# A mixture-of-experts kernel: two loads of x with their rows interleaved, and ScalarE's copy of h in two instructions for two experts

## The chip, the cores and the metric

The kernel runs on one core of one Trainium2 chip. A core has TensorE (PE) for matrix products, whose results lie in PSUM; ScalarE (ACT) and VectorE (DVE), which read PSUM and SBUF; GpSimd (POOL) and SyncE (SP), which here only issue transfers and pass on semaphores; and 16 DMA engines, which move data between HBM and SBUF. SBUF and PSUM have 128 partitions. The metric is the device time of one execution in microseconds: the median of the runs shown, before the change 180.69 us.

## The reference

Eight experts, each with 256 rows of x, 512 hidden columns and 2048 columns in between; everything is float32:

```python
n_experts, capacity, hidden, expert_hidden = 8, 256, 512, 2048
h = np.matmul(x, w1) + b1[:, np.newaxis, :]
h = np.maximum(h, 0)
out = np.matmul(h, w2) + b2[:, np.newaxis, :]
```

The weights w1 and w2 are 4 MB each for an expert, 64 MB in all, and the kernel reads each once.

## The kernel before

**Stages.** The kernel is written out by hand inside one critical section; each engine has its own list of instructions and they meet at semaphores. There are 11 stages, s = 0 to 10 (E + LAG, with LAG = 3). In stage s TensorE computes the first layer of expert s (for s below 8), and after it the second layer of expert s - 3 (from s = 3 on). The first layer is 16 rows of h (the loop over j; a row is here a block of 128 of the 2048 columns of h, transposed, for all 256 rows of x), each of four matmuls into one of four PSUM banks `ph`; the second layer is 32 matmuls into two banks `po`.

**Loads.** All weights are loaded by GpSimd, which converts them to fp16 on the way (`load_w1`, `load_w2`, lines 147 to 163), three buffers for w1 and three for w2 (NW). The order is fixed at lines 165 to 176: w1 of expert 0, b2, w1 of 1, x of 2 and 3, w1 of 2, w1 of 3, w2 of 0, x of 4 to 7, w1 of 4, w2 of 1, and so on. From expert 3 on, a load of w1 waits until TensorE has done the first layer that read the buffer (`s_ph`), and a load of w2 until the second layer is done (`s_po`). x of experts 0 and 1 alone comes as float32, in two transfers that SP issues before the critical section (line 131), ahead of the first weights: GpSimd's first load waits for a semaphore that ScalarE gives after its first small activation (line 127). SP then passes on, stage by stage, that x has been transposed and that weights have landed (`go`, lines 235 to 237 and 249 to 276), and TensorE takes that at line 282. Two stores of several experts' results and two of one expert's are issued by SP near the end (`flush`, `store`).

**x of experts 0 and 1.** 256 rows of 512 numbers lie one behind the other in HBM. Before the change partition p gets the two rows 2p and 2p + 1, which is 4 KB. (The change's short description counts such pairs of rows as one row.) VectorE casts expert 0 to fp16 and transposes it, ScalarE casts expert 1 (lines 133 to 135). `transposes` brings x to `xT` with 32 x 32 blocks; the columns of `xT` come in the order (row within the partition r, partition i).

**ScalarE's copy of h.** Line 224 adds the bias, takes the maximum with 0 and writes a row of h as fp16 into `hT`, and counts up `s_credit`; TensorE starts a row only with a credit, so it can be four rows ahead. The columns of `ph` are in the order of `xT`, and those of `hT` have to be in an order in which the results of a group of experts can be stored in long pieces (`GROUPS`: four experts together, then two). `h_columns` (line 206) gives the two access patterns, source and destination, for that. For experts 0 to 3 a partition of the group's result holds 8 rows (S), while a partition of x holds two rows (R) for experts 0 and 1, four for 2 and 3.

Of the kernel before, what the change touches and what calls it, by code (L numbers as in the profile page):

```python
# [10 lines left out]
def kernel(  # L11
# [12 lines left out]
    nc = tc.nc  # L24
    fp32 = mybir.dt.float32
    fp16 = mybir.dt.float16
    relu = mybir.ActivationFunctionType.Relu
    PE = mybir.EngineType.PE
    E, T, H = x.shape
    M = w1.shape[2]  # L30
    P = 128
    nTB = T // P
# [4 lines left out]
    B = 32  # L37
    nB = P // B
    LAG = 3
    NW = 3  # L40
    NPH = 4
    GROUPS = {0: 4, 4: 2}
# [6 lines left out]
    def sbuf(name, shape, dtype):  # L49
        return ctx.enter_context(nc.sbuf_tensor(name, shape, dtype))  # L50

    def sem(name):
        return ctx.enter_context(nc.semaphore(name=name))
# [3 lines left out]
    warm = sbuf("warm", [1, P], fp16)  # L57
    b2_sb = sbuf("b2_sb", [1, (LAG + E) * H], fp16)
    b1_rows = sbuf("b1_rows", [E * nB, M // nB], fp32)
    b1T = sbuf("b1T", [P, nJ * B + nB - 1], fp32)  # L60
    w1_sb = sbuf("w1_sb", [P, NW * nKC * M], fp16)
    w2_sb = sbuf("w2_sb", [P, NW * nJ * H], fp16)
    xT = sbuf("xT", [P, 2 * nKC * T], fp16)
    hT = sbuf("hT", [P, (LAG + 1) * nJ * T], fp16)
    x32 = [sbuf(f"x32_{e}", [P, nTB, H], fp32) for e in range(2)]
# [4 lines left out]
    for first, n in X_LOADS.items():  # L70
        R = n * T // P
# [9 lines left out]
    ph = ctx.enter_context(nc.psum_tensor("ph", [P, NPH, H], fp32))  # L81
# [5 lines left out]
    def load(engine, key, **kw):  # L87
        landed[key] = sem(f"d_{key}")
        engine.dma_start(**kw).then_inc(landed[key], 16)  # L89
# [4 lines left out]
    s_credit = sem("ph_free")  # L94
# [14 lines left out]
    def transposes(e):  # L109
# [19 lines left out]
        out=b1_rows[:], in_=b1.rearrange("e (b i) -> (e b) i", b=nB)))  # L129
    for e in range(2):  # L130
        tc.keep_in_program_order(nc.sync.dma_start(
            out=x32[e][:], in_=x[e].rearrange("(p tb) h -> p tb h", tb=nTB)))
    nc.vector.tensor_copy(out=x16[0][0][:], in_=x32[0][:])  # L133
    transposes(0)
    tc.keep_in_program_order(nc.scalar.copy(out=x16[1][0][:], in_=x32[1][:]))  # L135
# [12 lines left out]
    def load_w1(e):  # L148
        if e >= NW:
            nc.gpsimd.wait_ge(s_ph, nJ * (e - NW + 1))  # L150
        at = e % NW * nKC * M
        load(nc.gpsimd, f"w1_{e}",
             out=w1_sb[:, at : at + nKC * M].rearrange("p (kc m) -> p kc m", kc=nKC),
             in_=w1[e].rearrange("(p kc) m -> p kc m", kc=nKC))

    def load_w2(e):
        if e >= NW:
            nc.gpsimd.wait_ge(s_po, nTB * (e - NW + 1))
        dst = w2_sb[:, e % NW * nJ * H : (e % NW + 1) * nJ * H].rearrange("p (j h) -> p j h", j=nJ)
        src = w2[e].rearrange("(p j) h -> p j h", j=nJ)  # L160
        cuts = CUTS.get(e, (0, nJ))
        for lo, hi in zip(cuts, cuts[1:]):
            load(nc.gpsimd, f"w2_{e}_{lo}", out=dst[:, lo:hi], in_=src[:, lo:hi])

    nc.gpsimd.wait_ge(s_first, 1)
    load_w1(0)
    load(nc.gpsimd, "b2", out=b2_sb[:, LAG * H :],
         in_=b2.rearrange("e h -> (e h)").rearrange("(o f) -> o f", o=1))
    for s in range(1, E + LAG - 1):
        if s < E:  # L170
            if s in X_LOADS:
                load_x(s)
            load_w1(s)
        if s >= LAG:
            load_w2(s - LAG)
    load_w2(E - 1)
# [3 lines left out]
    for b in range(nB):  # L180
        turned = nc.vector.transpose(  # L181
            out=b1T[b * B : (b + 1) * B, nB - 1 - b : nB - 1 - b + nJ * B],
            in_=b1_rows[:].rearrange("r (i j) -> r j i", j=nJ),
# [3 lines left out]
    def evict(e, tb):  # L187
        engine = nc.vector if tb else nc.scalar
        copy = nc.vector.tensor_copy if tb else nc.scalar.copy
        first, n = group_of.get(e, (e, 1))  # L190
        rows = P // n
        at = (e - first) * rows
        engine.wait_ge(s_po, nTB * e + tb + 1)
        for k in range(n):
            bank = (e % 2 * nTB + tb) * H
            last = copy(out=results[e][at : at + rows, tb * n + k, :],  # L196
                        in_=po[k * rows : (k + 1) * rows, bank : bank + H])
        last.then_inc(s_out[tb], 1)
# [6 lines left out]

    def h_columns(e, dst, src):
        R, S = x16[e][2], group_of.get(e, (e, 1))[1] * nTB
        if R >= S:
            return (dst.rearrange("p (k i v) -> p k i v", k=S, v=R // S),
                    src.rearrange("p (v k i) -> p k i v", k=S, v=R // S))  # L210
        return (dst.rearrange("p (u r i) -> p u r i", r=R, u=S // R),
                src.rearrange("p (r i u) -> p u r i", r=R, u=S // R))

    nc.scalar.wait_ge(s_b1, 1)
    for s in range(E + LAG):
        if s < E:
            if s > LAG:
                nc.scalar.wait_ge(s_po, nTB * (s - LAG))
            for j in range(nJ):
                h_at = (s % (LAG + 1) * nJ + j) * T  # L220
                dst, src = h_columns(s, hT[:, h_at : h_at + T], ph[:, j % NPH, 0:T])
                bias_at = j * B + s * nB + nB - 1
                nc.scalar.wait_ge(s_ph, nJ * s + j + 1)
                nc.scalar.activation(  # L224
                    out=dst,
                    in_=src,
                    func=relu,
                    bias=b1T[:, bias_at : bias_at + 1],
                    scale=1.0,
                ).then_inc(s_credit, 1)  # L230
        if s >= LAG:
            evict(s - LAG, 0)

# [15 lines left out]
    for s in range(E + LAG):  # L249
# [5 lines left out]
        e = s - LAG  # L255
# [28 lines left out]
    def at(value, most):  # L284
        return nc.tensor.snap(value.with_bounds(min_val=0, max_val=most))

    with nc.Fori(0, E + LAG, 1, engines=[PE]) as s:
        nc.tensor.wait_ge(s_credit, NPH)
        w_at = at(s % NW * (nKC * M), (NW - 1) * nKC * M)
        with nc.tensor.If(s < E):  # L290
            x_at = at(s % 2 * (nKC * T), nKC * T)
            take(s_go)
            with nc.Fori(w_at, w_at + nJ, half, engines=[PE]) as w_from:
                w_from = w_from.with_bounds(min_val=0, max_val=(NW - 1) * nKC * M + half)
                for j in range(half):
                    for kc in range(nKC):
                        last = nc.tensor.matmul(  # L297
                            ph[:, j % NPH, 0:T],
                            w1_sb[:, bass.ds(w_from + (kc * M + j), P, nJ)],
                            xT[:, bass.ds(x_at + kc * T, T)],  # L300
                            start=(kc == 0),
                            stop=(kc == nKC - 1),
                        )
# [4 lines left out]
        with nc.tensor.If(s >= LAG):  # L308
            h_at = at((s + 1) % (LAG + 1) * (nJ * T), LAG * nJ * T)
# [3 lines left out]
            def second(tb, h_from, w2_from, j, stop=False):  # L313
                return nc.tensor.matmul(  # L314
                    banks[tb],
                    hT[:, bass.ds(h_from + (j * nTB + tb) * P, P)],
                    w2_sb[:, bass.ds(w2_from + j * H, H)],
                    start=False,
                    stop=stop,
                )  # L320
# [12 lines left out]
            for tb in range(nTB):  # L333
                for j in range(2 * TURN, nJ):
                    last = second(tb, h_at, w_at, j, stop=(j == nJ - 1))
# [36 lines left out]
```

## Time and profile before

| what | value |
|---|---|
| median of 3 runs | 180.69 us (180.69 to 180.79) |
| the profiled execution, device time | 180.71 us |
| its span in the profile | 178.9 us |
| PE matmul busy | 134.0 us, 75% |
| ACT busy | 75.6 us, 42%, 153 instructions |
| DVE busy | 65.0 us, 36% |
| granted TensorE clock, mean | 0.976 |
| DMA, moved into SBUF or out of it | 40.46 MB, mean 226 GB/s |
| HBM read, written | 71.39 MB, 4.19 MB |

How to read it: times inside the profile count from the start of the span; the device time is 1.8 us longer, for what lies around it. PEld is TensorE's weight load, which overlaps matmuls. Weights count in the DMA figures by the bytes that arrive (fp16), which is half of what is read. In the timeline each row has the start, the time from the first start to the last end, engine, line, operation, the program's names of output and inputs, the count, and in brackets how long the engine was idle before and what ended it; "PEq" is TensorE's own sequencer. L224 is line 224 of the kernel.

### The profile page before, as it was taken

Reading aid. Unit: us, or ns where it says so; the run is one execution under the profiler, and the core shown is the slowest. Engines: PE = TensorE matmul, PEld = TensorE weight load, DVE = VectorE, ACT = ScalarE, POOL = GpSimd, SP = SyncE. Lnnn points to the kernel's source line nnn. Section 1 sums busy time; section 2 is a strip of 40 time slices with the busy share of each in tenths; the row PEclk is TensorE's granted clock in tenths of the full one; section 3 lists DMA queues with packets and bytes.
Section 4 is the critical chain, followed back from the end, with each engine's and each line's share of the span. In section 5 each row is a group of like instructions: output and inputs, shape, how many; then the busy total and the mean of one; then the engine's idle time right before and its main releaser. Section 6 shows DMA issues by size and latency. Waiting matters only on the chain. (4 is left out here: it accounts for less than half of the span.)

```text
span 178.9 us, 2980 instructions
## 1 busy us (share of the span) xinstructions
PE 134.0 (75%) x784; PEld 93.0 (52%) x784; DVE 65.0 (36%) x92; ACT 75.6 (42%) x153; POOL 12.4 (7%) x26
## 2 busy tenths in 40 slices
PE   0003978868699890998968896989698896999960
PEld 0003878858689330894458543874298442433420
DVE  1989928475000289600097006910330003031010
ACT  3201786757777113582087505680387201021010
POOL 4300012020200101001010001000200003000000
PEclk9999999999999999699999999699999999999997
DMA  6999999999998999999999999899999999999996
GB/s 218 266 205 207 234 205 205 234 216 196 236 223 185 236 227 194 223 231 201 212 234 209 201 234 223 190 231 231 194 220 231 205 209 211 216 216 207 355 414 256
DMA packets 3970, 40.46 MB, mean 226 GB/s; under 512 B 464, under 2 KB 480, under 8 KB 1408
## 3 DMA queue, kind: packets, MB, share of 16 engines
q0 software_dynamic: 3056, 35.14, 92.7%
q1 hardware_dynamic: 864, 5.24, 7.2%
q10 hardware_dynamic: 48, 0.07, 0.1%
q14 instruction: 2, 0.02, 0.0%
HBM read 71.39 MB, written 4.19 MB: 422 GB/s over the span
## 5 line engine op out<-in xcount | busy, mean ns | idle before, releaser
L297 PE MATMUL ph<-xT,w_sb 128*128 x512 | 72.5, 303 | 33.0 <-PEq L282 30.5
L297 PEld LDWEIGHTS ph<-xT,w_sb 128*128 x512 | 66.6, 146 | 39.9 <-issue 31.4
L224 ACT ACTIVATE hT<-ph,b1T 128x256 f16<-128x256 f32 x128 | 60.2, 475 | 33.4 <-PE ph L297 29.9
L314 PE MATMUL po<-w_sb,hT 128*128 x256 | 56.7, 379 | 2.2 <-issue 2.2
L120 DVE STREAM_TRANSPOSE xT<-x 32x256 f16<-32x256 f16 (+2 forms) x64 | 45.0, 702 | 27.3 <-DMA x<-in_x_dram 22.7
L314 PEld LDWEIGHTS po<-w_sb,hT 128*128 x256 | 24.9, 97 | 33.0 <-issue 7.0
L196 DVE COPY out<-po 32x512 f32<-32x512 f32 (+1 forms) x20 | 13.7, 687 | 63.1 <-PE po L314 62.9
L196 ACT COPY out<-po 32x512 f32<-32x512 f32 (+1 forms) x20 | 11.6, 578 | 46.0 <-PE po L314 45.8
L89 POOL DMA_DIRECT2D w_sb<-in_w_dram x19 | 10.7, 567 | 136.9 <-PE po L314 71.7
L324 PE MATMUL po<-b_sb,ones 1*128 x16 | 4.8, 378 | 3.9 <-issue 2.5
L196 ACT COPY x<-po 128x512 f32<-128x512 f32 x2 | 1.2, 586 | 14.2 <-PE po L314 14.2
L196 DVE COPY x<-po 128x512 f32<-128x512 f32 x2 | 1.4, 692 | 13.9 <-PE po L314 13.9
L324 PEld LDWEIGHTS po<-b_sb,ones 1*128 1x128 f16 x16 | 1.4, 90 | 6.6 <-issue 6.3
L181 DVE STREAM_TRANSPOSE b1T<-b_rows 32x512 f32<-32x512 f32 x4 | 4.1, 1024 | 0.5 <-issue 0.5
L135 ACT CAST x<-x 128x1024 f16<-128x1024 f32 x1 | 1.0, 1046 | 3.2 <-DMA x<-in_x_dram 3.2
L133 DVE CAST x<-x 128x1024 f16<-128x1024 f32 x1 | 0.7, 694 | 2.9 <-DMA x<-in_x_dram 2.9
L127 ACT ACT_TABLE_LOAD x1 | 1.3, 1283 | 0.7 <-PEq L356 0.7
L89 POOL DMA_DIRECT2D x<-in_x_dram x2 | 1.1, 544 | 0.0
L89 POOL DMA_DIRECT2D b_sb<-in_b_dram x1 | 0.5, 509 | 0.0
L126 DVE MEMSET ones<- 1x128 f16 x1 | 0.2, 165 | 0.9 <-PEq L356 0.9
L127 ACT ACTIVATE warm<-ones 1x128 f16<-1x128 f16 x1 | 0.3, 308 | 0.0
L356 POOL MEMSET const-float32-0.0<- 128x1 f32 x1 | 0.1, 99 | 0.2 <-issue 0.2
(3 smaller groups left out, 0.3 us busy)
## 6 DMA issues: line engine op xcount, KB each, us to landing
w_sb<-in_w_dram POOLq DMA_DIRECT2D x14, 2048.0 KB, 41.1
w_sb<-in_w_dram POOLq DMA_DIRECT2D x3, 1024.0 KB, 25.0
out_dram<-out SPq DMA_DIRECT2D x1, 2048.0 KB, 7.3
x<-in_x_dram SPq DMA_DIRECT2D x2, 512.0 KB, 3.8
x<-in_x_dram POOLq DMA_DIRECT2D x1, 1024.0 KB, 34.3
w_sb<-in_w_dram POOLq DMA_DIRECT2D x2, 512.0 KB, 18.2
out_dram<-out SPq DMA_DIRECT2D x1, 1024.0 KB, 9.4
out_dram<-x SPq DMA_DIRECT2D x2, 512.0 KB, 7.2
```

The source lines that it names most:

```text
L89: engine.dma_start(**kw).then_inc(landed[key], 16)
L120: last = nc.vector.transpose(out=mine[b * B : (b + 1) * B].rearrange("p kc (r g i) -> p g r kc i", r=R, i=B)[:, g], in_=src[:, :, b * (H / ...
L126: nc.vector.memset(ones1[:], 1.0)
L127: tc.keep_in_program_order(nc.scalar.activation(out=warm[:], in_=ones1[:], func=relu).then_inc(s_first, 1))
L133: nc.vector.tensor_copy(out=x16[0][0][:], in_=x32[0][:])
L135: tc.keep_in_program_order(nc.scalar.copy(out=x16[1][0][:], in_=x32[1][:]))
L181: turned = nc.vector.transpose(out=b1T[b * B : (b + 1) * B, nB - 1 - b : nB - 1 - b + nJ * B], in_=b1_rows[:].rearrange("r (i j) -> r j i" ...
L196: last = copy(out=results[e][at : at + rows, tb * n + k, :], in_=po[k * rows : (k + 1) * rows, bank : bank + H])
L224: nc.scalar.activation(out=dst, in_=src, func=relu, bias=b1T[:, bias_at : bias_at + 1], scale=1.0,).then_inc(s_credit, 1)
L297: last = nc.tensor.matmul(ph[:, j % NPH, 0:T], w1_sb[:, bass.ds(w_from + (kc * M + j), P, nJ)], xT[:, bass.ds(x_at + kc * T, T)], start=(k ...
L314: return nc.tensor.matmul(banks[tb], hT[:, bass.ds(h_from + (j * nTB + tb) * P, P)], w2_sb[:, bass.ds(w2_from + j * H, H)], start=False, s ...
L324: nc.tensor.matmul(banks[tb], ones1[:], b2_sb[:, bass.ds(s * H, H)], start=True, stop=False)
```

## The change

The load of x for experts 0 and 1 takes the pairs of rows in another order. With NQ = 16, partition 8k + i gets pair i * 16 + k (k from 0 to 15, i from 0 to 7), where before it got pair 8k + i. Each partition still gets 4 KB that lie together in HBM, and there are still two transfers of 512 KB, on the same queue and at the same place. Eight neighbouring partitions now hold pairs that lie 64 KB apart, and partitions 8 apart hold neighbouring pairs.

With this the columns of `xT` and `ph` are in another order for these two experts. `hT` has to come out as before, so `h_columns` returns for them two pairs of access patterns, one for each r, of three dimensions each, u, i and v (four, eight and four elements). In the destination v lies closest together; in the source neighbouring v are 32 columns apart. ScalarE runs one activation of 128 columns for each r, and only the second counts up `s_credit`. For the other six experts `h_columns` returns a list with one pair, as before.

```diff
+    NQ = 16
...
     for e in range(2):
         tc.keep_in_program_order(nc.sync.dma_start(
-            out=x32[e][:], in_=x[e].rearrange("(p tb) h -> p tb h", tb=nTB)))
+            out=x32[e][:],
+            in_=x[e].rearrange("(i k tb) h -> k i (tb h)", k=NQ, tb=nTB)))
...
     def h_columns(e, dst, src):
         R, S = x16[e][2], group_of.get(e, (e, 1))[1] * nTB
+        if e < 2:
+            v = NQ * R // S
+            dst = dst.rearrange("p (u r i v) -> p r u i v", r=R, u=S // R, v=v)
+            src = src.rearrange("p (r v u i) -> p r u i v", r=R, u=S // R, v=v)
+            return [(dst[:, r], src[:, r]) for r in range(R)]
         if R >= S:
-            return (dst.rearrange("p (k i v) -> p k i v", k=S, v=R // S),
-                    src.rearrange("p (v k i) -> p k i v", k=S, v=R // S))
-        return (dst.rearrange("p (u r i) -> p u r i", r=R, u=S // R),
-                src.rearrange("p (r i u) -> p u r i", r=R, u=S // R))
+            return [(dst.rearrange("p (k i v) -> p k i v", k=S, v=R // S),
+                     src.rearrange("p (v k i) -> p k i v", k=S, v=R // S))]
+        return [(dst.rearrange("p (u r i) -> p u r i", r=R, u=S // R),
+                 src.rearrange("p (r i u) -> p u r i", r=R, u=S // R))]
...
-                dst, src = h_columns(s, hT[:, h_at : h_at + T], ph[:, j % NPH, 0:T])
                 bias_at = j * B + s * nB + nB - 1
                 nc.scalar.wait_ge(s_ph, nJ * s + j + 1)
-                nc.scalar.activation(
-                    out=dst,
-                    in_=src,
-                    func=relu,
-                    bias=b1T[:, bias_at : bias_at + 1],
-                    scale=1.0,
-                ).then_inc(s_credit, 1)
+                for dst, src in h_columns(s, hT[:, h_at : h_at + T], ph[:, j % NPH, 0:T]):
+                    last = nc.scalar.activation(
+                        out=dst,
+                        in_=src,
+                        func=relu,
+                        bias=b1T[:, bias_at : bias_at + 1],
+                        scale=1.0,
+                    )
+                last.then_inc(s_credit, 1)
```

## The prediction

> **What bounds the kernel now.** I read the page first, then the DMA share stretch by stretch, then the timeline of TensorE.
>
> ```profile
> span 178.9 us, 2980 instructions
> DMA  6999999999998999999999999899999999999996
> q0 software_dynamic: 3056, 35.14, 92.7%
> q1 hardware_dynamic: 864, 5.24, 7.2%
> DMA w_sb<-in_w_dram 22%; PE po L314 16%; PE ph L297 5%; PE po L324 1%; DVE x L196 0%; ACT hT L224 0%; SPq L237 0%; SPq L236 0%
> w_sb<-in_w_dram POOLq DMA_DIRECT2D x14, 2048.0 KB, 41.1
> ```
>
> The two large queues took 92.7% and 7.2% of sixteen engines' span: the DMA engines have almost no idle time. The chain of waits lists a weight transfer beside TensorE's second layer, but a transfer that takes 41.1 us from issue to landing was mostly queued. The windows say so directly (columns: the stretch, its length, busy us of PE, PEld, DVE, ACT, POOL, the granted clock, DMA share, GB/s):
>
> ```profile
> 5.30:168.00 162.70, 128.95 (x762) 90.99 (x763) 62.91 (x88) 73.44 (x150) 9.57 (x19) 0.98 1.02 216
> 168.00:177.00 9.00, 5.01 (x23) 2.04 (x21) 0.69 (x1) 0.59 (x1) 0.00 (x0) 1.00 0.99 416
> ```
>
> From 5.3 to 168 us the share is 1.02, and from 168 to 177, where the results are stored, 0.99. So the end is one sum: when the engines begin, how long the two x loads hold them, then weights, then stores, without a hole. TensorE matters only if it leaves such a hole, or delays the last store:
>
> ```profile
> 173.04 0.69 DVE L196 COPY x<-po 128x512 f32<-128x512 f32 x1 [7.36 <-PE po L314]
> out_dram<-x SPq DMA_DIRECT2D x2, 512.0 KB, 7.2
> DMA to landing us min/median/max: 4.2/8.4/10.1
> ```
>
> The last eviction ends at 173.7 us and its store (the quickest of the four) needs 4.2 us, to about 178. A store of 4.2 MB at 416 GB/s takes 10.1 us, and 168 + 10.1 is also 178: the store waits in line behind the other three.
>
> **The x loads.** They are two issues on SP's queue, ahead of every weight:
>
> ```profile
> 0.74 0.86 SPq L131 DMA_DIRECT2D x<-in_x_dram  x2
> 3.99 0.69 DVE L133 CAST x<-x 128x1024 f16<-128x1024 f32 x1 [2.91 <-DMA x<-in_x_dram]
> 5.54 1.05 ACT L135 CAST x<-x 128x1024 f16<-128x1024 f32 x1 [3.21 <-DMA x<-in_x_dram]
> 1.50:2.00 0.50, 0.00 (x0) 0.00 (x0) 0.00 (x0) 0.50 (x1) 0.00 (x0) 1.00 0.59 131
> 2.00:2.50 0.50, 0.00 (x0) 0.00 (x0) 0.00 (x0) 0.33 (x2) 0.00 (x0) 1.00 0.82 287
> 3.50:4.00 0.50, 0.00 (x0) 0.00 (x0) 0.01 (x1) 0.00 (x0) 0.50 (x2) 1.00 1.10 406
> 4.71 7.17 DVE L120 STREAM_TRANSPOSE xT<-x 32x256 f16<-32x256 f16 x16
> 16.11 9.80 PE L297 MATMUL ph<-xT,w_sb 128*128 x64 [16.11 <-PEq L282]
> q1 hardware_dynamic: 288, 1.05, 75.4%
> ```
>
> The last line is the DMA view of the stretch 1.5 to 5.3 us: 288 packets, 1.05 MB, 75.4% of 3.8 us, which is 2.87 us of each engine. The stores move such packets at 416 GB/s, and 1.05 MB at that rate is 2.52 us. The new order of rows changes neither bytes nor the 4 KB that each partition receives, so the best it can do is take away the difference, 2.87 - 2.52 = 0.35 us, which lies in the slow first microsecond (131, then 287 GB/s, against 406 later). The other bound: every engine halted by another at each packet, rate halved, 2.52 us more. Between these I take -0.1 us, a part of the ramp: the steady part runs at the store rate already, so a pattern can hardly help there, and reading 64 KB that lie together with all engines at once gives no reason in these rows to be slow. Both issues on SP together take 0.86 us. A source with one dimension more might double that, but the second would still be issued (0.74 + 1.72 = 2.5 us) while the first transfer runs (until 3.99), so it costs nothing unless the first issue also starts its transfer later, at most 0.43 us.
>
> When x lands matters to nothing else: the first transposes run on DVE from 4.7 us, and the first matmul is at 16.11, behind the first weights.
>
> **The second ScalarE instruction.** In stages 0 and 1 each of 16 rows gets two instructions of 128 columns in place of one of 256, so 32 more.
>
> ```profile
> L224 ACT ACTIVATE hT<-ph,b1T 128x256 f16<-128x256 f32 x128 | 60.2, 475 | 33.4 <-PE ph L297 29.9
> L196 ACT COPY out<-po 32x512 f32<-32x512 f32 x16 | 9.2, 577 | 30.3 <-PE po L314 30.2
> L135 ACT CAST x<-x 128x1024 f16<-128x1024 f32 x1 | 1.0, 1046 | 3.2 <-DMA x<-in_x_dram 3.2
> ```
>
> No 128-column instruction is shown. Bounds: half of 475, 237 ns, if nothing is fixed (then a row costs what it does now), and 475 ns, if nothing scales or the finer strides of the new pattern (runs of 4, not of 32) eat what is saved. From 512 to 1024 columns the two other rows grow by 469 ns, 0.92 ns a column, so 128 columns fewer are worth 117 ns: 475 - 117 = 358 ns. With some 35 ns between rows, as now (8 in 4.06 us, below), I take 0.75 us a row; the bounds are 0.51 and 1.0.
>
> ```profile
> 17.25 0.47 ACT L224 ACTIVATE hT<-ph,b1T 128x256 f16<-128x256 f32 x1 [10.66 <-PE ph L297]
> 20.38 1.79 ACT L224 ACTIVATE hT<-ph,b1T 128x256 f16<-128x256 f32 x4 [0.16 <-PE ph L297]
> 22.32 4.11 ACT L224 ACTIVATE hT<-ph,b1T 128x256 f16<-128x256 f32 x8
> 26.21 1.06 POOL L89 DMA_DIRECT2D w_sb<-in_w_dram  x2 [20.34 <-PE ph L297]
> 27.48 4.38 PE L297 MATMUL ph<-xT,w_sb 128*128 x32 [1.57 <-PEq L282]
> 28.31 4.06 ACT L224 ACTIVATE hT<-ph,b1T 128x256 f16<-128x256 f32 x8 [1.89 <-PE ph L297]
> 33.16 4.10 ACT L224 ACTIVATE hT<-ph,b1T 128x256 f16<-128x256 f32 x8 [0.79 <-PE ph L297]
> 38.32 4.35 PE L297 MATMUL ph<-xT,w_sb 128*128 x32 [1.57 <-PEq L282]
> ```
>
> Behind ScalarE stands TensorE, which may be four rows ahead (four banks of ph) and then waits for credits. Stage 0: the activations start 17.25 us in, and by 20.38 four of them had begun, one in 0.8 us, so TensorE sets the pace there; then 12 rows take 9.0 us, to 29.4; now ScalarE is done at 26.4 (22.32 + 4.11): +3.0. Stage 1 begins 1.05 us after that, as it does now (27.48), its first activation 0.83 us later (now 28.31) at 31.3, and 16 rows end at 43.3, in place of 37.3 (33.16 + 4.10): +6.0. Stages 2 and 3 keep their length, so the lag on entering stage 4 would be 6.0 us. With 1.0 us a row the same steps give 33.3 and 51.1: 13.8.
>
> What hides it:
>
> ```profile
> 71.84 9.41 PE L297 MATMUL ph<-xT,w_sb 128*128 x64 [4.95 <-PEq L282]
> 91.22 4.40 PE L297 MATMUL ph<-xT,w_sb 128*128 x32 [1.53 <-PEq L282]
> 110.58 9.29 PE L297 MATMUL ph<-xT,w_sb 128*128 x64 [1.62 <-PEq L282]
> 129.96 4.40 PE L297 MATMUL ph<-xT,w_sb 128*128 x32 [1.65 <-PEq L282]
> 149.08 0.60 PE L324 MATMUL po<-b_sb,ones 1*128 x2 [1.40 <-SPq L237]
> L290 PEldq COMPARE_BRANCH  x1: 74/74/74, 108.3 to 108.3; - x1
> L237 SPq EVENT_SEMAPHORE  x1: 9561/9561/9561, 100.4 to 100.4; - x1
> ```
>
> In each of these five places TensorE is idle until weights have landed. That the idle time is slack and not loop overhead shows in the last two rows, for stage 6: TensorE's sequencer has passed its branch at 108.4 us, before the last matmul ended, while SP's wait for the weights lasts until 100.4 + 9.56 = 110.0. So the slack is 4.95, then 1.53, 1.62, 1.65 and 1.40, together 11.1 us. A lag of 6.0 is 1.1 after the first and gone before stage 5 has begun.
>
> The lag must also leave no hole in the DMA stream. GpSimd issues the weights of expert 3 when stage 0 has let go of their buffer (26.21 us now, about 29 then), and the stream still has the weights of experts 1 and 2 and a load of x ahead of it. Later issues wait the same way: with four transfers in line (41.1 us to landing against 9.6 each, the length of SP's wait above) a lag of 6 us, or 13.8, leaves the line filled. DVE's next transposes wait for s_ph too, and SP's go for them, both before stage 2's and 3's matmuls, which are late anyway. Cost: 0.
>
> A larger ScalarE program may need one more instruction fetch. In the DMA view of 41 to 47 us two such packets stand:
>
> ```profile
> q14 instruction: 2, 0.02, 0.7%
> ```
>
> 0.7% of 6 us on 16 engines is 0.67 us, 0.34 a packet, on one engine; landing waits for the slowest. So 0 to +0.34; 32 instructions are a small part of one, and I take 0.
>
> **Sum.** 178.9 - 0.1 + 0 + 0 = 178.8 us of span. The profiled execution took 180.71 with 1.8 us around its span, and the median is 180.69, so the two agree: 180.6 us, no change that a measurement of this kernel can tell (0.2%, 0.36 us).
>
> **Rivals.**
>
> The x loads become slower (the other side). If the new source splits the 128 partitions over the engines so that two of them write through one way into the memory at a time, the loads run at half rate: +1.26 us for the first alone, should the engines drift apart, +2.52 for both. Every microsecond goes into the unbroken stream and to the end: 182.0 to 183.2. Against it: today's 406 GB/s in the middle of the load. For it: the first microsecond, in which something holds the engines up, and it decides as soon as more than a seventh of the load is lost.
> The Trainium skill speaks for this one. In "SBUF — State Buffer" (Door 1: The DMA port swizzle) partitions 0-3 and 32-35 share a port, and "DMA: Bandwidth & Descriptors" (The descriptor swizzle; and on how k is chosen) gives each engine of a plain 128-partition transfer the partitions of one port. An outermost dimension of 16 may instead hand engine k the partitions 8k to 8k+7, so that in step engines k and k+4 meet at one port. No row here shows which partitions an engine writes, and by this rule the time would be the one just given.
>
> ScalarE costs more than the slack: a lag over 11.1 us. Now ScalarE's rows take 9.2 us in stage 0 and 8.9 in stage 1, so with 32 rows at p the lag is 32p - 18.1, and p must exceed 0.91 us, each half over 0.44. At 1.0 us 13.8 - 11.1 = 2.7 us remain, 183.3 at most, about 182.5 if the last store is then less held up by the others. For it: strides never tried here. Against: all eight experts, with two strides, have the same 475 ns.
>
> The ramp goes away entirely: -0.35 us, and the engines start more evenly, so the slowest gains a little more than the mean, some 0.5 us: 180.2.
>
> **How the numbers follow.** Forecast 0.52 (180.3 to 181.0 by the bounds of ramp and fetch); slower x loads 0.25; ScalarE over its slack 0.07; ramp gone 0.16. Faster is the last, 0.16; slower the two before it, 0.32; same 0.52. The range runs from 180.1, under the fast case, to 182.4, which takes in half of the slow loads and leaves out about 0.15.
>
> **What would show it.** The stretch 1.5 to 5.3 us: q1's share of it stays near 75% (right), or goes toward 66% (ramp gone) or over 80% (conflict). ScalarE's group of 128 x 128 shows 64 instructions near 360 ns. Stage 4's first matmul stays near 72 us with less idle time before it, and those at 91.22, 110.58, 129.96 and 149.08 do not move by more than the x loads do. The DMA share from 5.3 to 168 us stays at 1.0; a stretch below that, or a landing of weights that shifts later than the loads of x did, would make the prediction wrong.

## The result, and the profile after

The changed kernel takes 182.6 us (median of 5 runs, 182.5 to 182.75) against 180.71: a ratio of 1.0103, 95% interval 1.0091 to 1.0114. It is slower by 1.9 us, outside the range of the prediction (up to 182.4) and on the other side of its forecast. The profiled execution took 182.5 us, with a span of 180.7; before it was 180.71 and 178.9.

From the page of the changed kernel, the span, the DMA share in 40 slices and the queues:

```profile
span 180.7 us, 3012 instructions
DMA  5999999999999999999999989999999999999996
q0 software_dynamic: 3056, 35.14, 91.7%
q1 hardware_dynamic: 864, 5.24, 7.9%
q14 instruction: 3, 0.02, 0.0%
```

The stream is as unbroken as before, but its first slice is 5 in place of 6, the queue of x and of the stores (q1) took 7.9% in place of 7.2%, and a third instruction fetch (q14) has come. Now the loads of x, from the DMA view of 1.5 to 7.1 us and the windows (start, length, busy us of five engines, clock, DMA share, GB/s):

```profile
q1 hardware_dynamic: 288, 1.05, 76.7%
...
1.50:2.00 0.50, 0.00 (x0) 0.00 (x0) 0.00 (x0) 0.50 (x1) 0.00 (x0) 1.00 0.00 0
2.50:3.00 0.50, 0.00 (x0) 0.00 (x0) 0.00 (x0) 0.00 (x0) 0.36 (x1) 1.00 0.81 303
3.50:4.00 0.50, 0.00 (x0) 0.00 (x0) 0.00 (x0) 0.00 (x0) 0.50 (x2) 1.00 1.02 279
4.50:5.00 0.50, 0.00 (x0) 0.00 (x0) 0.00 (x0) 0.00 (x0) 0.50 (x2) 1.00 1.00 221
```

The same 288 packets and 1.05 MB took 76.7% of 5.6 us, 4.30 us of each engine, where they had taken 2.87: 1.43 us more. In the two later windows the engines are fully busy (share 1.02 and 1.00) and move 279 and 221 GB/s, where before they moved 406. And nothing moves before 2.0 us, where before 131 GB/s were under way: in the packet records the first one starts at 2.18 us in place of 1.76, 0.42 later. Start and packets together are 1.85 us. Where that goes, from the timeline:

```profile
0.74 1.29 SPq L132 DMA_DIRECT2D x<-in_x_dram  x2
5.73 0.69 DVE L135 CAST x<-x 128x1024 f16<-128x1024 f32 x1 [4.65 <-DMA x<-in_x_dram]
7.91 1.04 ACT L137 CAST x<-x 128x1024 f16<-128x1024 f32 x1 [5.58 <-DMA x<-in_x_dram]
17.82 10.13 PE L305 MATMUL ph<-xT,w_sb 128*128 x64 [17.82 <-PEq L290]
24.00 5.28 ACT L231 ACTIVATE hT<-ph,b1T 128x128 f16<-128x128 f32 x20 [0.20 <-PE ph L305]
41.44 4.35 PE L305 MATMUL ph<-xT,w_sb 128*128 x32 [1.58 <-PEq L290]
73.41 9.29 PE L305 MATMUL ph<-xT,w_sb 128*128 x64 [3.41 <-PEq L290]
92.83 4.40 PE L305 MATMUL ph<-xT,w_sb 128*128 x32 [1.68 <-PEq L290]
112.16 4.40 PE L305 MATMUL ph<-xT,w_sb 128*128 x32 [1.60 <-PEq L290]
131.57 9.29 PE L305 MATMUL ph<-xT,w_sb 128*128 x64 [1.67 <-PEq L290]
150.90 0.60 PE L332 MATMUL po<-b_sb,ones 1*128 x2 [1.60 <-SPq L245]
```

The first matmul is 1.71 us late (17.82 against 16.11), because the weights are. TensorE at stage 2 is 3.1 us late, at stage 4 only 1.57, and from there on 1.61, 1.58, 1.61 and 1.82: everything after the first weights has moved by nearly one and the same shift, and TensorE still waits for weights at each of these places. The further 1.4 us at stage 2 are absorbed: at stage 4 TensorE waits 3.41 us where it had waited 4.95. Most of them are probably not ScalarE's. With the new load alone and with ScalarE's part alone (both kernels are below) stage 2 is 1.66 and 0.19 us late, which leaves some 1.3 us, and the windows of the changed kernel show a low clock just then:

```profile
30.00:34.00 4.00, 3.92 (x20) 3.17 (x21) 3.93 (x6) 2.31 (x8) 0.00 (x0) 0.58 0.98 209
```

The granted clock, the column before the DMA share, is 0.58 over these 4 us, in which TensorE got through only 20 matmuls. Before the change it is 1.00 in this stretch, with 27 matmuls.

### The profile page after: what moved, and what is told of

It is laid out like the page before. It is cut to its first block, busy times and chain, and to the rows that moved or that the text cites. A ratio compares the mean times of both kernels' runs of the same rounds, so it can differ in the third digit from the quotient of the medians.

```text
span 180.7 us, 3012 instructions
## 1 busy us (share of the span) xinstructions
PE 135.1 (75%) x784; PEld 93.4 (52%) x784; DVE 65.1 (36%) x92; ACT 78.2 (43%) x185; POOL 12.0 (7%) x26
## 5 line engine op out<-in xcount | busy, mean ns | idle before, releaser
L305 PE MATMUL ph<-xT,w_sb 128*128 x512 | 73.7, 309 | 33.4 <-PEq L290 31.4
L231 ACT ACTIVATE hT<-ph,b1T 128x256 f16<-128x256 f32 (+1 forms) x160 | 62.8, 449 | 30.1 <-PE ph L305 27.8
```

The source lines that it names most:

```text
L231: last = nc.scalar.activation(out=dst, in_=src, func=relu, bias=b1T[:, bias_at : bias_at + 1], scale=1.0,)
L305: last = nc.tensor.matmul(ph[:, j % NPH, 0:T], w1_sb[:, bass.ds(w_from + (kc * M + j), P, nJ)], xT[:, bass.ds(x_at + kc * T, T)], start=(k ...
```

## The experiments

**The load alone, and ScalarE alone.** One kernel has the new load and the old single activation:

```diff
-            out=x32[e][:], in_=x[e].rearrange("(p tb) h -> p tb h", tb=nTB)))
+            out=x32[e][:],
+            in_=x[e].rearrange("(i k tb) h -> k i (tb h)", k=16, tb=nTB)))
```

> The new load of x, with ScalarE's one instruction a row as before; the rows of experts 0 and 1 therefore come out in another order. If the load alone carries the loss: 182.6 us, the same q1 share in the stretch 1.5 to 5.3 us and w1 of expert 0 landing about 1.7 us later than before. If the second ScalarE instruction has a part in it (a lag of TensorE's first two stages that reaches the end): less than 182.3 us.

The other has the old load and two activations in stages 0 and 1:

```diff
+                halves = [(dst[:, :, r], src[:, :, r]) for r in range(nTB)] if s < 2 else [(dst, src)]
+                for d, c in halves:
+                    last = nc.scalar.activation(
+                        out=d,
+                        in_=c,
...
+                last.then_inc(s_credit, 1)
```

> The old load, and two ScalarE instructions of 128 columns a row in stages 0 and 1 (each half takes the columns of one r). If the lag is hidden by TensorE's waits for weights: 180.7 us, stage 2 some 3 us later than before and stage 5 where it was. If ScalarE carries the loss: 182 us or more.

The load alone: 182.66 us, 1.0107 (1.009 to 1.0124). ScalarE alone: 180.92 us, 1.0005 (0.9995 to 1.0014), no difference. The whole loss is in the load: with the new load alone TensorE begins 1.66 us late and is 1.80 or 1.81 us late at each of the five places where it waits for weights. From the kernel with ScalarE's part alone, a group of instructions and the timeline:

```profile
L226 ACT ACTIVATE hT<-ph,b1T 128x128 f16<-128x128 f32 x64 | 17.4, 405 | 13.6 <-PE ph L300 13.6
28.50 4.24 ACT L226 ACTIVATE hT<-ph,b1T 128x128 f16<-128x128 f32 x16 [1.65 <-PE ph L300]
38.51 4.35 PE L300 MATMUL ph<-xT,w_sb 128*128 x32 [1.57 <-PEq L285]
72.00 9.54 PE L300 MATMUL ph<-xT,w_sb 128*128 x64 [4.92 <-PEq L285]
```

A half lasts 405 ns, but sixteen of them fit into 4.24 us: the next starts 0.26 us after the last, while that is still running (64 of them are busy for only 17.4 us). So a row of two takes 0.53 us, hardly more than the 0.51 of a row of one, and stage 2 begins 0.2 us later than before (38.51 against 38.32), not the 3 us that were expected. The changed kernel's own finer strides cost little more: its 20 halves in the row at 24.00 us take 5.28 us, 0.26 each as well.

**Which side of the transfer.** The first question was whether the order in HBM slows the packets (16 engines on neighbouring pieces) or the new shape of the transfer. This kernel has the shape of the change, but eight neighbouring partitions read one stretch of HBM (32 KB), as they did before:

```diff
-            out=x32[e][:], in_=x[e].rearrange("(p tb) h -> p tb h", tb=nTB)))
+            out=x32[e][:],
+            in_=x[0:2].rearrange("e (k j i tb) h -> j (e k) i (tb h)", k=8, j=2, i=8, tb=nTB)[e]))
```

> The load keeps the changed shape (16 by 8 pieces of 4 KB, the source's steps not mergeable), but partition 8k+i now gets pair 16k+i of experts 0 and 1 together (expert 1's tile: pair 16k+8+i), so the pieces of eight neighbouring partitions lie together in HBM as before the change; the tiles of experts 0 and 1 hold other rows than they should. If the order in HBM (neighbouring pieces 8 partitions apart) is what slows the packets: mean packet back near 178 ns, about 181.1 us with only the later start left. If the outer dimension of 16 does it, by how partitions are shared out or how descriptors are made: packets near 266 ns, 182.6 us.

And this one a third dimension, but 128 outermost:

```diff
+            out=x32[e][:], in_=x[e].rearrange("(tb p) h -> p tb h", tb=nTB)))
```

> The load's outer dimension is 128 again, but of three dimensions: partition p gets row p and row p + 128, two pieces of 2 KB (rows of experts 0 and 1 come out in another order). If a third dimension by itself makes descriptors slow: q1's time in the load well above before's 2.85 us an engine and about 182 us or more. If the shape of 128 partitions outermost is what keeps the engines apart: time as before in the packets, 180.7 to 181.2 us, the later start possibly kept.

With the shape kept and neighbouring pieces in neighbouring partitions: 182.99 us, 1.0119 (1.0102 to 1.0135). With 128 outermost: 181.16 us, 1.0019 (1.0009 to 1.0028). In the DMA views, of 1.5 to 7.1 us for the first, of 1.5 to 5.6 us for the second, and the second's issues:

```profile
q1 hardware_dynamic: 282, 1.04, 75.9%
```

```profile
q1 hardware_dynamic: 544, 1.05, 74.9%
0.74 0.95 SPq L131 DMA_DIRECT2D x<-in_x_dram  x2
```

75.9% of 5.6 us is 4.25 us, as slow as the change: the order in HBM is not the cause. 74.9% of 4.1 us is 3.07 us, though there are twice as many pieces of half the size: three dimensions are not the cause either. What is left is the outer dimension of 16.

**Ports, or the making of descriptors.** Two explanations were left. Either each of 16 engines now gets eight neighbouring partitions, and engines meet at the ports of the memory, or descriptors for such a shape come too slowly. Four kernels were made to tell them apart. Two of them were to leave fewer engines at work (k = 2, and k = 4):

```diff
+            out=x32[e][:],
+            in_=x[e].rearrange("(i k tb) h -> k i (tb h)", k=2, tb=nTB)))
```

> The load's source has an outer dimension of 2 (partition 64k+i gets pair i*2+k; rows of experts 0 and 1 in another order), which by either theory leaves 2 engines at work, one on partitions 0 to 63, the other on 64 to 127. If two engines that write partitions of one port halve each other (0-3 with 32-35 and so on, 64 and above apart): these two never meet, packets of 4 KB near 159 ns, the two loads done in about 20 us. If the way descriptors are made for such a shape is slow: packets as slow as in the changed kernel, near 266 ns.

> The same with an outer dimension of 4: 4 engines, of which the first two write partitions 0 to 31 and 32 to 63, the others 64 to 95 and 96 to 127 (rows of experts 0 and 1 in another order). If engines meet at ports: both pairs meet at every step, packets near 300 ns, the loads take as long as with 2 engines or little less. If descriptors are the limit: packets as in outer_2.

Their times (215.75 and 206.89 us) only say that x came late; what counts is a packet. From the DMA views of 8 to 40 us of the kernel with 2 and of that with 4:

```profile
q1 hardware_dynamic: 66, 0.27, 2.2%
```

```profile
q1 hardware_dynamic: 133, 0.53, 4.3%
```

2.2% of 32 us on 16 engines, over 66 packets, is 171 ns each, so nothing in the shape slows a packet when two engines work apart. (In the packet records of the first microseconds two packets of x are under way at a time in the first kernel and four in the second.) With 4 engines it is 166 ns, and here the expectation of the ports failed: they were to meet in pairs. In that stretch the queue of the weights takes most of the time (89.2% and 90.2% in the same views), so two engines may seldom be at the same step. Before the weights start, ten of the first sixteen packets took 159 or 160 ns in the packet records and the others 320 to 1232; engines that are so far apart after one packet may not meet later. The records don't name the engine, so this stays open. And the loads last until 55 us with 2 engines and 46 with 4, not the 20 expected, beside the weights that those engines also move.

The next kernel leaves shape and order alone and loads the halves of the tiles one after the other:

```diff
-    for e in range(2):
+    for lo in (0, P // 2):
+        for e in range(2):
...
+                out=x32[e][lo : lo + P // 2],
+                in_=x[e].rearrange("(p tb) h -> p tb h", tb=nTB)[lo : lo + P // 2]))
```

> The old order of rows and the old two-dimensional shape, but each tile in two transfers of 64 partitions, first both tiles' lower halves, then both upper halves. If engines meet at ports: 64 partitions have 8 of the 16 ports, so 16 engines share them in pairs and packets take near 300 ns, 182 us or more. If only the outer dimension of 16 with its third dimension is slow to describe: packets near 165 ns, and less than 181.5 us (two issues more).

And the fourth gives each partition a piece of 8 KB, both experts in one transfer, with the outer dimension of 16:

```diff
...
+    tc.keep_in_program_order(nc.sync.dma_start(
+        out=x32_both[:],
+        in_=x[0:2].rearrange("e t h -> (e t) h").rearrange("(i k r) h -> k i (r h)", k=16, i=8)))
```

> Both experts in one transfer with the outer dimension of 16 by 8, each partition getting 8 KB that lie together (tiles of experts 0 and 1 hold other rows): the same bytes, half the pieces. If ports limit: the bytes take as long as in the changed kernel, some 4.2 us of each engine. If the making of descriptors limits: about 2.5 to 2.9 us of each engine, because each brings twice as much.

The halves: 182.51 us, 1.009 (1.0061 to 1.0119). The 8 KB pieces: 183.03 us, 1.0118 (1.0089 to 1.0148). The DMA view of 1.5 to 7.1 us of the latter:

```profile
q1 hardware_dynamic: 128, 1.05, 78.4%
```

With half the pieces the engines needed 78.4% of 5.6 us, 4.39 us: bytes limit, not the number of descriptors. So the making of descriptors is out, and for the ports one more kernel loads 64 partitions as half_tiles does, but others, 32 to 95 first:

```diff
+    for lo, hi in ((B, P - B), (0, B), (P - B, P)):
+        for e in range(2):
...
+                out=x32[e][lo:hi],
+                in_=x[e].rearrange("(p tb) h -> p tb h", tb=nTB)[lo:hi]))
```

> As half_tiles, the old order and two-dimensional shape, but the tiles' partitions 32 to 95 first, for both experts, then 0 to 31, then 96 to 127. If it is the port that counts (0-3 shares with 32-35 and so on, 64 and above apart), partitions 32 to 95 hold one partition group of each of the 16 ports: the first 128 packets near 165 ns, though the transfers are of 64 partitions as in half_tiles; those after, 32 partitions at a time, near 300 ns. If transfers of 64 partitions are slow for another reason: the first 128 packets near 320 ns as well.

The windows of the halves' kernel with its DMA view of 3.5 to 5.0 us, then those of this one with its view of 2.8 to 4.2 us:

```profile
3.50:4.00 0.50, 0.00 (x0) 0.00 (x0) 0.00 (x0) 0.00 (x0) 0.50 (x2) 1.00 0.82 172
4.00:4.50 0.50, 0.00 (x0) 0.00 (x0) 0.00 (x0) 0.00 (x0) 0.50 (x2) 1.00 1.27 246
4.50:5.00 0.50, 0.00 (x0) 0.00 (x0) 0.00 (x0) 0.00 (x0) 0.50 (x2) 1.00 0.78 156
...
q1 hardware_dynamic: 78, 0.25, 84.5%
```

```profile
3.00:3.50 0.50, 0.00 (x0) 0.00 (x0) 0.00 (x0) 0.00 (x0) 0.50 (x2) 1.00 1.01 397
3.50:4.00 0.50, 0.00 (x0) 0.00 (x0) 0.00 (x0) 0.00 (x0) 0.50 (x2) 1.00 1.09 397
...
q1 hardware_dynamic: 128, 0.44, 85.9%
```

Partitions 0 to 63 take in 156 to 246 GB/s, 191 over these three windows; partitions 32 to 95, in transfers of the same size and shape, 397. (The windows next to them, where a transfer begins or ends, have 336 in the first kernel and 287 in the second.) Of the packets in the two views 62 and 107 carry 4 KB, the others 4 bytes: 84.5% of 1.5 us on 16 engines is 327 ns for each of the 62, and 85.9% of 1.4 us is 180 ns for each of the 107, near the 300 and the 165 that were expected if the ports count. The packet records of the halves' kernel show it once more: from 2.4 to 3.1 us, with some eight of its packets under way at a time, 28 of 35 took 165 ns or less; from 3.4 to 5.0 us, with mostly sixteen under way, 69 of 72 took over 280. Which partitions are written together decides, and by a factor of about two. That is what the Trainium skill says in "SBUF — State Buffer" (Door 1: The DMA port swizzle): 0 to 63 reach half of the ports, 32 to 95 all of them. The kernel's time (184.25 us, 1.0184, 1.0131 to 1.0237) says nothing on that; the transfers behind the first two took turns with the weights and came late, so its first matmul was at 25.6 us. (In the halves' kernel it was at 20.77, so that kernel's time is not the price of the packets either.) The packets behind the first 128, 32 partitions at a time, were expected near 300 ns; in the records their median is 172. That part of the expectation failed; these packets come between those of the weights and say nothing for or against the ports.

**Another number in the change.** If eight neighbouring partitions for one step of the outer dimension are the trouble, four may not be. In the changed kernel:

```diff
-    NQ = 16
+    NQ = 32
```

> The changed kernel with NQ = 32: partition 4k+i gets pair i*32+k, four neighbouring partitions for each step of the outer dimension. If with an outer dimension other than 128 each engine gets eight neighbouring partitions and engines meet in pairs: as the changed kernel, packets near 266 ns, 182.6 us. If four neighbouring partitions can be shared out as a plain load's are: packets near 178 ns, 180.9 to 181.2 us, the later start left.

181.71 us, 1.0047 (1.0032 to 1.0061), half of the loss gone. Its DMA view of 1.5 to 7.1 us, its issues and its first matmul:

```profile
q1 hardware_dynamic: 288, 1.05, 49.2%
0.74 1.27 SPq L132 DMA_DIRECT2D x<-in_x_dram  x2
16.78 5.06 PE L305 MATMUL ph<-xT,w_sb 128*128 x32 [16.78 <-PEq L290]
```

49.2% of 5.6 us is 2.76 us: the packets are as fast as before the change, or faster (2.87). What is left comes before them: the two issues take 1.27 us in place of 0.86 and the first packet starts at 2.15 us, so the first matmul is 0.67 late. The rest, up to 0.9 us in span, arises late in the kernel: TensorE is 0.65 late at 130.61 us and 0.90 at 149.98. A third instruction fetch lies between the two (below); whether it is the cause is not shown. So the expectation's mechanism held, and its time was 0.5 us too low. It is slower than the kernel before, and none of the versions tried is faster.

**How much ScalarE could take.** The old load and four activations of 64 columns a row in stages 0 and 1:

```diff
+                parts = [(dst[:, u : u + 2, r], src[:, u : u + 2, r])
+                         for r in range(nTB) for u in range(0, 4, 2)] if s < 2 else [(dst, src)]
```

> The old load and four ScalarE instructions of 64 columns a row in stages 0 and 1. With 0.26 us from one to the next, as two a row showed, a row takes 1.05 us and the lag at stage 4 is 32 times 1.05 less 18.1, 15 us: 11 of it hidden by the five waits for weights, up to 4 us at the end, 182 to 185 us. If they get shorter with their columns (0.2 us): a row of 0.8 us, lag 7.5 us, gone before stage 6, 180.7 to 180.9 us.

180.91 us, 1.0006 (0.9995 to 1.0016): no difference. Its timeline:

```profile
17.21 13.30 ACT L227 ACTIVATE hT<-ph,b1T 128x64 f16<-128x64 f32 x64 [10.49 <-PE ph L301]
75.11 4.68 PE L301 MATMUL ph<-xT,w_sb 128*128 x32
93.19 4.67 PE L301 MATMUL ph<-xT,w_sb 128*128 x32
111.27 4.67 PE L301 MATMUL ph<-xT,w_sb 128*128 x32
130.15 4.40 PE L301 MATMUL ph<-xT,w_sb 128*128 x32 [0.87 <-PEq L286]
```

Sixteen rows take 13.3 us, 0.83 a row. This is the expectation's second case, instructions that get shorter with their columns. The prediction's formula gives a lag of 32 x 0.83 - 18.1 = 8.5 us (stage 3 begins 8.15 late, 57.27 against 49.12), less 4.95 at stage 4 leaves 3.5. Against the starts of before (71.84, 91.22, 110.58, 129.96) the stages are 3.27, 1.97, 0.69 and 0.19 late: TensorE gets back 1.3 us in stage 4 and again in stage 5, no longer waits at stages 4, 5 and 6 (no bracket), and waits again at stage 7. Here the cover can be seen at work. About two of its 11.1 us were left: the 0.87 at stage 7, and 1.44 at the fifth place (149.31 us).

## Why the prediction was wrong

**What bounds the kernel** was right. One sum of DMA time, from first packet to last store, explains both kernels: a start 0.42 us later and packets that take 1.43 us more make 1.85, and the span grew by 1.8.

**The step that failed** is the one on the loads of x: "Between these I take -0.1 us". Of its two bounds (0.35 us gained, 2.52 us lost) the true value, 1.43 lost, is on the losing side and past the middle. The reason given, that reading 64 KB which lie together gives no reason to be slow, looked at one end of the transfer only. same_shape shows that this end, HBM, made no difference (4.25 us of each engine against 4.30), and half_tiles with mid_tiles that the other end, which partitions are written together, can halve the rate. The rival named that mechanism and its price, 1.26 to 2.52 us for the packets, and it is the rival that came about; it had a chance of 0.25. What spoke for it stood in the prediction and was outweighed by "today's 406 GB/s in the middle of the load", which says nothing on the new shape, since it was measured with the old one. That the changed kernel gives each engine eight neighbouring partitions, so that engines meet, is not shown directly; it is what is left, since the order in HBM, the third dimension and the number of pieces were each ruled out by a run, and NQ = 32 is free of it. The kernel with 4 engines, whose packets stayed at 166 ns, does not fit it without a further assumption.

**The issue** was bounded rightly ("at most 0.43 us" if the first transfer starts later) and then valued at nothing. The two issues took 1.29 us in place of 0.86, and the first packet came 0.42 later, in this kernel as in load_only. The range was built without that term: the rival's two ends plus it are 182.4 to 183.6, and the result lies inside.

**ScalarE's second instruction** costs the end nothing, as forecast, and act_only shows it. The size was wrong: 0.75 us a row was expected and 0.53 measured, since two activations one behind the other overlap by about a third (405 ns long, 0.26 us apart). So the lag of 6.0 us at stage 4 did not come either: what ScalarE itself adds is 0.2 us at stage 2 in act_only. The slack that was to hide it is real, but smaller than the 11.1 us counted: act_four got back 1.30 and 1.28 us in two stages where waits of 1.53 and 1.62 had been read, and in the next the last 0.50 with 0.87 of 1.65 to spare. The fifth wait, at 149.08 us before, was not touched, so where the cover ends was not tried.

**The instruction fetch** was bounded at 0 to 0.34 us and taken as 0. A third fetch came in each of the four profiles with 3012 instructions or more (the change, act_only, outer_32, act_four) and in none of the nine with fewer than 3000, where there are two. In the changed kernel it stands between 130 and 142 us, and the lateness there goes from 1.61 to 1.82 us. That is no proof of a price: load_only has two fetches, is 1.80 or 1.81 late all along, and has the same span and time (180.7 and 182.66 us). In act_only and act_four a price can't be told from the scatter of the runs. So the cost of a third fetch is not shown.

**The sign that was proposed** (q1's share of 1.5 to 5.3 us over 80% in a conflict) would have missed it: the changed kernel has 78.4% there, since a slow load isn't over by then. The share of a fixed stretch has to go with what was moved in it.

## What to carry to other kernels

When a transfer's access pattern changes, look at both of its ends, and at how its outermost dimension may divide the partitions over the engines: the same bytes in the same piece sizes took one and a half times as long here. In a kernel whose DMA engines are never idle, such a loss goes to the end undiminished (1.85 us in the load, 1.8 in the span), even in a load whose own consumer has time to spare, while a lag of TensorE by several microseconds, as in act_four, can vanish in its waits for weights. And a rate that was measured with the old shape is weak evidence against a mechanism that only the new shape would bring.

## What had not been expected of the hardware

The activations with a bias overlap strongly: 128 columns last 405 ns in the records and follow each other at 0.26 us, 64 columns last 440 and follow at 0.21 (13.3 us for 64). A duration from the profile is not the price of one more instruction; the distance from start to start comes nearer to it. And two transfers of 512 KB that only two or four engines carried lasted until 55 and 46 us beside a stream of weights: with two engines 66 packets of x got through in 32 us, 33 an engine, though one takes 0.17 us.
